# Where the output projection's products stand: moving six units' share into the last attention unit's steps

## The chip, the cores and the metric

The kernel runs on one core of a Trainium2 chip. The metric is the device time of one execution in microseconds (us). A core has TensorE (matrix products, called PE in the profile; its weight loads are PEld), VectorE (DVE), ScalarE (ACT), GpSimd (POOL) and SyncE (SP), which here only issues transfers. Each engine works through its own queue in order; semaphores hold an instruction until its inputs are there and its output buffer is free.

## The reference

A decoder trunk of two layers over 1024 tokens of width 1024, float32. Layer 1 uses differential attention with 8 heads ("units"), layer 2 forgetting attention with 16 heads (8 units of two heads). Each layer ends in a gated MLP. What matters here is the end of each attention stage: the heads' outputs, side by side, are multiplied by an output matrix, normalised and added to the stream.

```python
# layer 1
o = jnp.concatenate(outs, axis=1)
o = rms_norm(o, subln_g, SUBLN_EPS) * (1.0 - lambda_init)
a = o.reshape(B, S, A_HEADS * 2 * A_HEAD_DIM).astype(x.dtype) @ w_o
h = h + rms_norm(a, a_norm_post[l])
# layer 2
a = o.reshape(B, S, B_HEADS * B_HEAD_DIM).astype(x.dtype) @ w_o
h = h + rms_norm(a, b_norm_post[j])
f = conv_ffn(rms_norm(h, ffn_norm_pre[l]), ffn_w_in[l], ffn_conv_w[l], ffn_conv_b[l], ffn_w_out[l])
h = h + rms_norm(f, ffn_norm_post[l])
```

## The kernel before, in words

**Split products.** A float32 product is made of three products in a faster format (`fp32r`): each operand is split into a high part (a copy, by ScalarE) and a low part (the difference, by VectorE or GpSimd), and high x high, high x low and low x high are summed in PSUM. So a weight or an activation costs one ScalarE copy and one subtraction before it can be used.

**PSUM** has eight banks of 128 x 512 floats. In an attention stage the scores use banks 0 to 3, the transposes 4 and 5; projections and the products with the values ("PV") take the banks in the list `mlast`.

**An attention stage** is a loop over steps, written out by `go`. Layer 1 (`attention_a`) has 64 steps, 8 per unit, one for each block of 128 query rows, smallest first. Layer 2 (`attention_b`) has 128 steps, 8 per head and 16 per unit, the largest block first. In step n the kernel issues: the scores and softmax of block n (`front`), the transposes of block n-2 and their evacuation in two parts (`turn`), in every other step PV for a pair of blocks (`pv`), then filling work (`fill`), then what stands in `todo` for this step. This is program order; a scheduler that works at compile time lays each engine's queue in this order as priority, and brings a later instruction forward where it reckons that an earlier one is not ready.

**The filling work** (`plan`) is the query, key and value projections of later units, in pieces of 12 products 512 wide (`qk_pieces`, line 690) or 24 products 256 wide (`v_pieces`, line 757). Unit 7 is the last; its eight pieces are numbers 72 to 79, and line 902 puts them from step 48 (layer 1) or 96 (layer 2) on: one piece a step in layer 1, steps 49 to 55, and one every two steps in layer 2, steps 96 to 110.

**The output projection** is the products of 8 token blocks (128 rows each) with 8 units' rows of the matrix: per block and unit 6 products 512 wide (three parts, two column halves), 384 in a layer, all at line 464. `output_plan` puts its beginning into `todo`. Here `first` is the last unit's first step (56 in layer 1, 112 in layer 2), `n` the number of steps (64, 128) and `per` the steps of a unit (8, 16).

- `begin` sets `mlast = [4, 5]` and loads the norm's gain.
- `weight` asks for one of the eight weight tiles, evenly over the last unit. A weight is loaded into one of two raw buffers (`wr`), and split into two tiles of the pool `x`. That pool has 16 tiles, and the stage's own transposed input fills all 16 until the last projection has read it.
- The units' outputs lie in DRAM (`o_dram`); `out_load` fetches them for a token block (`oraw`), `out_split` splits them, `out_mm` issues products.
- Block 0 gets its products with units 0 to 5 during the last unit's steps, one unit every `per // 8` steps.
- Blocks 1 to 3 get theirs at step n + 4, behind the last PV in program order, and unit 6's products for blocks 0 to 3 come there too: 108 + 24 products.
- The last unit's own output goes through a reciprocal (layer 1: a norm), a row written to DRAM, that row read back to all partitions, and a scaling (`a_norm`, lines 1051 to 1071; `b_scale`, lines 1217 to 1235). It stays on the chip (`o_last`).
- `output_rest` then goes through the 8 blocks: unit 7's products for blocks 0 to 3, all 48 products for blocks 4 to 7. `post` follows for each block: square, gain, norm, addition to the stream; and after the later blocks the transposes for the MLP.

Of the kernel before, what the change touches and what calls it, by code (L numbers as in the profile page):

```python
# [95 lines left out]
class Kernel:  # L96
# [310 lines left out]
    def output_plan(self, gpost, h_in, h_out, gain, n, per):  # L407


        nc = self.nc  # L410
        self.todo = {}
        o = self.out_state = {"w": [], "raw": {}, "part": {}}

        def begin():
            self.mlast = [4, 5]
            o["post"] = self.make_post(gpost, h_in, h_out, False)

        def weight():
            o["w"].append(self.w.next(far=1))

        at = lambda step, *f: self.todo.setdefault(step, []).extend(f)
        first = n - per
        at(first, begin)
        for k in range(8):
            at(first + k * per // 8, weight)
        for tb in range(4):
            at(first + per // 4, lambda tb=tb: self.out_load(tb, 0, 6))
        eng = nc.gpsimd if per == NB else nc.vector
        at(first + 3 * per // 8, lambda: self.out_split(0, 0, 6, eng))
        for j in range(6):  # L430
            at(first + (3 + j) * per // 8, lambda j=j: self.out_mm(0, j, j + 1))
        at(n - 2, *[lambda tb=tb: self.out_load(tb, 6, 7) for tb in range(4)])
        for tb in range(1, 4):
            at(n - 2 + tb, lambda tb=tb: self.out_split(tb, 0, 6, nc.gpsimd))
        at(n + 4, *[lambda tb=tb: self.out_split(tb, 6, 7, nc.vector) for tb in range(4)])
        at(n + 4, *[lambda tb=tb: self.out_mm(tb, 0, 6) for tb in range(1, 4)])
        at(n + 4, *[lambda tb=tb: self.out_mm(tb, 6, 7) for tb in range(4)])

    def out_load(self, tb, c0, c1):
        r = self.out_state["raw"]  # L440
        if tb not in r:
            r[tb] = self.tile("oraw", shape=[P, 7, P])
        self.nc.sync.dma_start(
            out=r[tb][:, c0:c1], in_=self.o_dram[c0:c1, :, tb * P:(tb + 1) * P].rearrange("h p t -> p h t")
        )

    def out_split(self, tb, c0, c1, eng):
        nc, s = self.nc, self.out_state
        if tb not in s["part"]:
            s["part"][tb] = tuple(self.tile("o" + n, F32R, [P, 8, P], tag="w") for n in "hl")  # L450
        oh, ol = s["part"][tb]
        src = self.o_last[:, tb * P:(tb + 1) * P].unsqueeze(1) if c0 == 7 else s["raw"][tb][:, c0:c1]
        nc.scalar.copy(out=oh[:, c0:c1], in_=src)
        eng.tensor_tensor(out=ol[:, c0:c1], in0=src, in1=oh[:, c0:c1], op=ALU.subtract)

    def out_mm(self, tb, j0, j1):
        nc, s = self.nc, self.out_state
        oh, ol = s["part"][tb]
        b = 2 * ((tb + 3) % 4)
        for j in range(j0, j1):  # L460
            wh, wl = s["w"][j]
            for i, (o, wt) in enumerate(((oh, wh), (oh, wl), (ol, wh))):
                for c in range(2):
                    nc.tensor.matmul(  # L464
                        self.bank(b + c), o[:, j], wt[:, 0, c * HALF:(c + 1) * HALF],
                        start=j == 0 and i == 0, stop=j == 7 and i == 2,
                    )

    def output_rest(self, gain):
        nc, s = self.nc, self.out_state  # L470
        self.x_tag = "t"
        for tb in range(NB):
            if tb + 4 < NB:
                self.out_load(tb + 4, 0, 7)
            if tb < 4:
                self.out_split(tb, 7, 8, nc.vector)
                self.out_mm(tb, 7, 8)
            else:
                self.out_split(tb, 0, 7, nc.vector)
                self.out_split(tb, 7, 8, nc.vector)  # L480
                self.out_mm(tb, 0, 8)
            s["raw"].pop(tb)
            s["part"].pop(tb)
            if tb == 5:
                self.w.make(self.w.used + 2)
            s["post"](tb, self.ps[:, 2 * ((tb + 3) % 4) * HALF:2 * ((tb + 3) % 4) * HALF + D])
            if tb > 4:
                self.early(gain, tb - 4, (6, 0, 2))
        self.mlast = [6, 7]


# [389 lines left out]
    def plan(self, n_steps, start, layer_b):  # L881

        out = {}
        last = -1
        per = n_steps // 4
        pre = 4 if layer_b else 0
        for p in range(4):
            f = []
            for u in (2 * p + 1, 2 * p + 2):
                if u < 8:  # L890
                    f.append((u, None))
            if p < 3:
                f.append((None, p + 1))
            for i in range(8 * len(f)):
                u, v = f[i // 8]
                k = 24 * p + i
                if k < pre:
                    step = -1
                elif k < 72:
                    step = start + (k - pre) * 3 * per // (72 - pre)  # L900
                else:
                    step = 3 * per + (k - 72) * per // 16
                last = max(last, step)
                out.setdefault(last, []).append((u, v, i % 8))
        made = {}

        def emit(step):
            for u, v, i in out.get(step, []):
                if (u, v) not in made:
                    if u is None:  # L910
                        made[u, v] = self.v_pieces(v, layer_b)
                    else:
                        qk = self.qk_pieces(u)
                        made[u, v] = [x for which in "qk" for half in (0, 1) for x in qk[which, half]]
                made[u, v][i]()

        return emit
# [517 lines left out]
```

## Time and profile before

| What | Value |
|---|---|
| Median of 3 runs | 2557.89 us (2554.6 to 2558.18) |
| Profiled execution | 2557.8 us, of which the span is 2555.9 us |
| TensorE busy | 2495.0 us, 98% |
| VectorE, ScalarE, GpSimd busy | 1628.0, 1145.0, 853.1 us |
| Granted TensorE clock, mean | 0.996 |
| Last two units of layer 1 | about 381 to 487 us from the span's start |
| Last two units of layer 2 | about 1679 to 1798 us |

The page of the profile lists each engine's busy time, then the chain of work that ended last, then the costliest groups of instructions by line. A view by stretch gives the busy time of every engine between two moments; a view of waits says which engine stood idle for whom; a view in order of time lists single instructions with start and length. "L464" is line 464 of the kernel. A product counts as busy from its issue to a modelled end, so a busy TensorE is not a TensorE at its full pace.

### The profile page before, as it was taken

Reading aid. Unit: us, or ns where it says so; the run is one execution under the profiler, and the core shown is the slowest. Engines: PE = TensorE matmul, PEld = TensorE weight load, DVE = VectorE, ACT = ScalarE, POOL = GpSimd, SP = SyncE. Lnnn points to the kernel's source line nnn. Section 1 sums busy time; section 2 is a strip of 40 time slices with the busy share of each in tenths; the row PEclk is TensorE's granted clock in tenths of the full one; section 3 lists DMA queues with packets and bytes.
Section 4 is the critical chain, followed back from the end, with each engine's and each line's share of the span. In section 5 each row is a group of like instructions: output and inputs, shape, how many; then the busy total and the mean of one; then the engine's idle time right before and its main releaser. Section 6 shows DMA issues by size and latency. Waiting matters only on the chain.

```text
span 2555.9 us, 33917 instructions
## 1 busy us (share of the span) xinstructions
PE 2495.0 (98%) x12876; PEld 2118.3 (83%) x12876; DVE 1628.0 (64%) x2334; ACT 1145.0 (45%) x1949; POOL 853.1 (33%) x1057
## 2 busy tenths in 40 slices
PE   8999999999999999999999999997999999999998
PEld 8898998788788888888878888885887888888887
DVE  6767676568777877252556666666468777775243
ACT  5555555455333434242445555556344443434231
POOL 1222222226554550010334444435236455430000
PEclk9999999999999999999999999999999999999999
DMA  4111211441222225363311212224412222235363
GB/s 166 44 44 45 62 52 47 132 163 57 85 90 83 74 93 197 108 210 119 119 59 50 59 59 63 69 37 128 145 66 99 83 75 98 76 116 182 123 206 115
DMA packets 119864, 248.98 MB, mean 97 GB/s; under 512 B 34035, under 2 KB 50196, under 8 KB 119700
## 3 DMA queue, kind: packets, MB, share of 16 engines
q1 hardware_dynamic: 119700, 246.81, 29.5%
q8 instruction: 101, 1.65, 0.3%
q14 instruction: 63, 0.52, 0.1%
HBM read 197.85 MB, written 48.92 MB: 97 GB/s over the span
## 4 chain that ended last, share of the span: by engine, by line
PE 85%; DVE 7%; ACT 2%; DMA 2%; issue 2%; POOL 1%; SPq 0%; DVEq 0%; ACTq 0%; POOLq 0%
PE ps L581 28%; PE ps L293 18%; PE ps L690 13%; PE ps L757 7%; PE ps L464 6%; PE ps L836 3%; PE ps L1207 2%; PE ps L1035 2%; PE ps L806 2%; PE ps L805 2%; PE ps L565 1%; DVE y L612 1%; DVE wl L81 1%; DVE tl L555 1%; DMA wr<-in_b_o_dram 1%
## 5 line engine op out<-in xcount | busy, mean ns | idle before, releaser
L81 DVE TENSOR_TENSOR wl<-wr,wh 128x1024 fp32r<-128x1024 f32 x160 | 202.6, 1267 | 282.2 <-ACT wh L79 275.7
L293 PE MATMUL ps<-wh,src 128*128 128x512 f32 x1408 | 377.2, 389 | 0.0
L79 ACT CAST wh<-wr 128x1024 fp32r<-128x1024 f32 x164 | 172.2, 1052 | 337.2 <-PE ps L293 238.4
L293 PEld LDWEIGHTS ps<-wh,src 128*128 128x128 f32 x1408 | 264.1, 188 | 55.1 <-issue 0.2
L581 PE MATMUL ps<-xq,sh 128*128 128x512 f32 x912 | 281.3, 390 | 2.0 <-ACT e L589 2.0
L610 ACT ACTIVATE y<-ps,conv 128x1024 f32<-128x1024 f32 x88 | 106.2, 1207 | 370.9 <-DVE ps L586 369.0
L612 DVE SCALAR_TENSOR_TENSOR y<-ps,conv,y 128x1023 f32<-128x1023 f32 (+1 forms) x176 | 224.8, 1278 | 55.1 <-ACT y L610 51.2
L293 PE MATMUL ps<-wl,src 128*128 128x512 f32 x704 | 216.8, 389 | 0.0
L817 POOL CAST qz<-qs 64x128 fp32r<-64x128 f32 x256 | 82.6, 324 | 391.2 <-PE ps L806 340.3
L210 POOL TENSOR_SCALAR post<-post 128x1 f32<-128x1 f32 x56 | 21.4, 382 | 569.0 <-ACT f L214 568.6
L690 PE MATMUL ps<-xh,wh 128*128 128x512 f32 x512 | 207.4, 405 | 1.4 <-DVE qs L711 0.7
L516 POOL TENSOR_TENSOR sl<-ws,sh 128x1024 fp32r<-128x1024 f32 x38 | 105.5, 2776 | 303.2 <-ACT sh L515 303.2
L581 PEld LDWEIGHTS ps<-xq,sh 128*128 128x128 f32 x912 | 170.9, 188 | 38.6 <-ACT e L589 3.4
L690 PE MATMUL ps<-xh,wl 128*128 128x512 f32 x512 | 201.2, 393 | 0.0
L690 PE MATMUL ps<-xl,wh 128*128 128x512 f32 x512 | 201.2, 393 | 0.0
L847 DVE TENSOR_TENSOR ptl<-ps,pth 128x512 fp32r<-128x512 f32 (+3 forms) x288 | 152.6, 553 | 65.8 <-ACT pth L846 64.5
L581 PE MATMUL ps<-th,sh 128*128 128x512 f32 x456 | 177.6, 390 | 2.0 <-DVE f L586 2.0
L581 PE MATMUL ps<-tl,sh 128*128 128x512 f32 x456 | 177.4, 389 | 0.0
L581 PE MATMUL ps<-xq,sl 128*128 128x512 f32 x456 | 177.4, 389 | 0.0
L581 PE MATMUL ps<-th,sl 128*128 128x512 f32 x456 | 177.4, 389 | 0.0
L846 ACT CAST pth<-ps 128x512 fp32r<-128x512 f32 (+3 forms) x288 | 130.5, 478 | 60.7 <-PE ps L836 56.5
L293 PEld LDWEIGHTS ps<-wl,src 128*128 128x128 f32 x704 | 132.2, 188 | 27.3
(197 smaller groups left out, 6152.3 us busy)
## 6 DMA issues: line engine op xcount, KB each, us to landing
wr<-in_ffn_in_dram SPq DMA_DIRECT2D x88, 512.0 KB, 3.5
wr<-in_ffn_out_dram SPq DMA_DIRECT2D x88, 512.0 KB, 3.6
g<-y SPq DMA_DIRECT2D x44, 512.0 KB, 2.8
g<-g SPq DMA_DIRECT2D x44, 512.0 KB, 6.6
h<-hold SPq DMA_DIRECT2D x24, 512.0 KB, 2.9
hold<-h SPq DMA_DIRECT2D x24, 512.0 KB, 6.8
crow<-c SPq DMA_DIRECT2D x16, 512.0 KB, 8.4
xraw<-in_x_dram SPq DMA_DIRECT2D x8, 512.0 KB, 6.6
```

What stands on the lines that cost most here:

```text
L79: self.k.nc.scalar.copy(out=hi[:, :size], in_=raw[:, :size])
L81: eng.tensor_tensor(out=lo[:, :size], in0=raw[:, :size], in1=hi[:, :size], op=ALU.subtract)
L293: nc.tensor.matmul(self.bank(2 * t + c), s[:, sp, t * P:(t + 1) * P], wt[:, 0, c * HALF:(c + 1) * HALF], start=first and wt is wh and sp = ...
L464: nc.tensor.matmul(self.bank(b + c), o[:, j], wt[:, 0, c * HALF:(c + 1) * HALF], start=j == 0 and i == 0, stop=j == 7 and i == 2,)
L516: (eng or nc.vector).tensor_tensor(out=lo, in0=raw, in1=hi, op=ALU.subtract)
L581: nc.tensor.matmul(o, w[wi][:, k], x[k][xi], start=start and k == 0 and i == 0, stop=k == 3 and i == 2, skip_group_check=not start,)
L610: nc.scalar.activation(out=y, in_=ps, func=AF.Identity, scale=cw[:, 2:3], bias=cw[:, 3:4])
L612: nc.vector.scalar_tensor_tensor(out=y[:, k:], in0=ps[:, :S - k], scalar=cw[:, 2 - k:3 - k], in1=y[:, k:], op0=ALU.mult, op1=ALU.add)
L690: nc.tensor.matmul(self.bank(b), w[:, kc], x[kc][:, c], start=kc == 0 and i == 0, stop=kc == 7 and i == 2)
L757: nc.tensor.matmul(o, x[kc][:, tb * P:(tb + 1) * P], w[:, kc % 4], start=kc == 0 and i == 0, stop=kc == 7 and i == 2,)
L846: nc.scalar.copy(out=hi, in_=src)
L847: nc.vector.tensor_tensor(out=lo, in0=src, in1=hi, op=ALU.subtract)
```

## The change

Three things are changed, in both layers.

1. **Unit 7's projections** are made two pieces at a time: the divisor at line 902 goes from 16 to 32. They end at step 51 in layer 1 and at step 103 in layer 2.
2. **Blocks 0 to 3 with units 0 to 5** are now 16 groups of 18 products (`out_part`: a block, a column half, three units). All are summed in bank 7; after the second group of a column half ScalarE copies the bank into a tile `osum`. In layer 1 two groups go to each of the steps 59 to 66, in layer 2 one to each of 112 to 127. `begin` comes three or seven steps ahead of the last unit and leaves PV bank 6 alone. Weights are asked for at given steps: six of them by step 57 in layer 1, five by step 111 and six by step 112 in layer 2. The loads of blocks 0 to 3 go into tiles of the pool `x`, all four at step 57 in layer 1, one to a step from 107 to 110 in layer 2. The splits are GpSimd's in layer 1 and VectorE's in layer 2, where blocks 1 to 3 were GpSimd's.
3. **Behind the last PV**, at step n + 4, only block 4 is issued ahead, with units 0 to 6 (42 products). In `output_rest` blocks 0 to 3 get the products of units 6 and 7 (12 each) in another bank pair, and VectorE adds `osum`. Units 6 and 7 of these blocks are split 512 columns at a time.

```diff
     def output_plan(self, gpost, h_in, h_out, gain, n, per):
...
         def begin():
-            self.mlast = [4, 5]
+            self.mlast = [6]
             o["post"] = self.make_post(gpost, h_in, h_out, False)
 
         def weight():
-            o["w"].append(self.w.next(far=1))
+            o["w"].append(self.w.next(far=2))
...
         first = n - per
-        at(first, begin)
-        for k in range(8):
-            at(first + k * per // 8, weight)
+        wide = per == NB
+        eng = self.nc.gpsimd if wide else self.nc.vector
+        step = lambda b, x: first + (x if wide else b)
+        at(step(-7, -3), begin)
+        for j, b, x in ((0, -7, -3), (1, -6, -3), (2, -4, -2), (3, -3, -1), (4, -1, 0), (5, 0, 1), (6, 7, 5), (7, 11, 7)):
+            at(step(b, x), weight)
         for tb in range(4):
-            at(first + per // 4, lambda tb=tb: self.out_load(tb, 0, 6))
-        eng = nc.gpsimd if per == NB else nc.vector
-        at(first + 3 * per // 8, lambda: self.out_split(0, 0, 6, eng))
-        for j in range(6):
-            at(first + (3 + j) * per // 8, lambda j=j: self.out_mm(0, j, j + 1))
-        at(n - 2, *[lambda tb=tb: self.out_load(tb, 6, 7) for tb in range(4)])
-        for tb in range(1, 4):
-            at(n - 2 + tb, lambda tb=tb: self.out_split(tb, 0, 6, nc.gpsimd))
-        at(n + 4, *[lambda tb=tb: self.out_split(tb, 6, 7, nc.vector) for tb in range(4)])
-        at(n + 4, *[lambda tb=tb: self.out_mm(tb, 0, 6) for tb in range(1, 4)])
-        at(n + 4, *[lambda tb=tb: self.out_mm(tb, 6, 7) for tb in range(4)])
+            at(step(-5 + tb, 1), lambda tb=tb: self.out_load(tb, 6, "x"))
+        for tb, b, x in ((0, -2, 2), (1, 3, 3), (2, 6, 5), (3, 10, 6)):
+            at(step(b, x), lambda tb=tb: self.out_split(tb, 6, eng))
+        for i in range(16):
+            at(step(i, 3 + i // 2), lambda i=i: self.out_part(i // 4, i // 2 % 2, i % 2))
+        at(n - 1 if wide else n - 4, self.out_load_last)
+        at(n if wide else n - 2, lambda: self.out_load(4, 7, "t"))
+        at(n + 4, lambda: self.out_split_last(0))
+        at(n + 4, lambda: self.out_split(4, 7, self.nc.vector))
+        at(n + 4, lambda: self.out_mm(4, 0, 7))
...
+    def out_part(self, tb, c, third):
+        nc, s = self.nc, self.out_state
+        oh, ol = s["part"][tb]
+        for j in range(3 * third, 3 * third + 3):
+            self.out_products(7, (oh[:, j], ol[:, j]), j, c, j == 0, j == 5)
+        if third == 0:
+            return
+        if c == 0:
+            s["sum"][tb] = self.tile("osum")
+        nc.scalar.copy(out=s["sum"][tb][:, c * HALF:(c + 1) * HALF], in_=self.bank(7))
+        if c == 1:
+            s["part"].pop(tb)
+
+    def out_bank(self, tb):
+        return (6, 4, 6, 4, 0, 2, 6, 4)[tb]
...
     def output_rest(self, gain):
...
+        self.out_split_last(1)
         for tb in range(NB):
-            if tb + 4 < NB:
-                self.out_load(tb + 4, 0, 7)
+            b = self.out_bank(tb)
+            ps = self.ps[:, b * HALF:b * HALF + D]
+            if tb in (1, 2, 3):
+                self.out_load(tb + 4, 7, "t")
             if tb < 4:
-                self.out_split(tb, 7, 8, nc.vector)
-                self.out_mm(tb, 7, 8)
+                oh, ol = s["late"]
+                t = slice(tb * P, (tb + 1) * P)
+                for j in (6, 7):
+                    for c in range(2):
+                        self.out_products(b + c, (oh[:, j - 6, t], ol[:, j - 6, t]), j, c, j == 6, j == 7)
+                o = s["sum"].pop(tb)
+                nc.vector.tensor_tensor(out=o, in0=ps, in1=o, op=ALU.add)
+                ps = o
             else:
-                self.out_split(tb, 0, 7, nc.vector)
-                self.out_split(tb, 7, 8, nc.vector)
-                self.out_mm(tb, 0, 8)
+                if tb > 4:
+                    self.out_split(tb, 7, nc.vector)
+                    self.out_mm(tb, 0, 7)
+                self.out_split_one(tb)
+                self.out_mm(tb, 7, 8)
...
@@ plan
-                    step = 3 * per + (k - 72) * per // 16
+                    step = 3 * per + (k - 72) * per // 32
```

More of the change, by code (lines that the diff above doesn't have):

```diff
@@ L407, in output_plan @@
     def output_plan(self, gpost, h_in, h_out, gain, n, per):
-        nc = self.nc
         self.todo = {}
-        o = self.out_state = {"w": [], "raw": {}, "part": {}}
+        o = self.out_state = {"w": [], "raw": {}, "part": {}, "sum": {}}
         def begin():
-            self.mlast = [4, 5]
+            self.mlast = [6]
             o["post"] = self.make_post(gpost, h_in, h_out, False)
         def weight():
-            o["w"].append(self.w.next(far=1))
+            o["w"].append(self.w.next(far=2))
@@ L432, in output_plan @@
-        at(n - 2, *[lambda tb=tb: self.out_load(tb, 6, 7) for tb in range(4)])
-        for tb in range(1, 4):
-            at(n - 2 + tb, lambda tb=tb: self.out_split(tb, 0, 6, nc.gpsimd))
-        at(n + 4, *[lambda tb=tb: self.out_split(tb, 6, 7, nc.vector) for tb in range(4)])
-        at(n + 4, *[lambda tb=tb: self.out_mm(tb, 0, 6) for tb in range(1, 4)])
-        at(n + 4, *[lambda tb=tb: self.out_mm(tb, 6, 7) for tb in range(4)])
[L439 to L442, printed above, removed]
+        wide = per == NB
@@ new lines, in output_plan, with out_load @@
+        for i in range(16):
[5 more added lines that the diff above has]
+        at(n + 4, lambda: self.out_mm(4, 0, 7))
+    def out_load(self, tb, n, tag):
+        r = self.out_state["raw"][tb] = self.tile("oraw", shape=[P, n, P], tag=tag)
@@ L443, in out_load, with out_split @@
         self.nc.sync.dma_start(
-            out=r[tb][:, c0:c1], in_=self.o_dram[c0:c1, :, tb * P:(tb + 1) * P].rearrange("h p t -> p h t")
+            out=r, in_=self.o_dram[0:n, :, tb * P:(tb + 1) * P].rearrange("h p t -> p h t")
         )
-    def out_split(self, tb, c0, c1, eng):
+    def out_split(self, tb, n, eng):
         nc, s = self.nc, self.out_state
[L449 to L454, printed above, removed]
@@ L456, in out_mm, with out_split_one @@
-    def out_mm(self, tb, j0, j1):
+        src = s["raw"].pop(tb)
+        oh, ol = s["part"][tb] = tuple(self.tile("o" + x, F32R, [P, 8, P], tag="w") for x in "hl")
+        nc.scalar.copy(out=oh[:, :n], in_=src)
+        eng.tensor_tensor(out=ol[:, :n], in0=src, in1=oh[:, :n], op=ALU.subtract)
+    def out_split_one(self, tb):
+        nc = self.nc
+        oh, ol = self.out_state["part"][tb]
+        src = self.o_last[:, tb * P:(tb + 1) * P]
+        nc.scalar.copy(out=oh[:, 7], in_=src)
+        nc.vector.tensor_tensor(out=ol[:, 7], in0=src, in1=oh[:, 7], op=ALU.subtract)
@@ new lines, in out_load_last, with out_split_last @@
+    def out_load_last(self):
+        r = self.out_state["raw6"] = self.tile("oraw6", shape=[P, HALF])
+        self.nc.sync.dma_start(out=r, in_=self.o_dram[6, :, 0:HALF])
+    def out_split_last(self, i):
+        nc, s = self.nc, self.out_state
+        if i == 0:
+            s["late"] = tuple(self.tile("o" + x, F32R, [P, 2, HALF], tag="w") for x in "hl")
+        oh, ol = s["late"]
+        src = s.pop("raw6") if i == 0 else self.o_last[:, 0:HALF]
+        nc.scalar.copy(out=oh[:, i], in_=src)
+        nc.vector.tensor_tensor(out=ol[:, i], in0=src, in1=oh[:, i], op=ALU.subtract)
@@ L457, in out_mm, with out_products @@
+    def out_products(self, bank, o, j, c, start, stop):
+        wh, wl = self.out_state["w"][j]
+        oh, ol = o
+        for i, (x, wt) in enumerate(((oh, wh), (oh, wl), (ol, wh))):
+            self.nc.tensor.matmul(
+                self.bank(bank), x, wt[:, 0, c * HALF:(c + 1) * HALF], start=start and i == 0, stop=stop and i == 2
+            )
+    def out_part(self, tb, c, third):
         nc, s = self.nc, self.out_state
         oh, ol = s["part"][tb]
-        b = 2 * ((tb + 3) % 4)
@@ L460, in out_mm @@
-        for j in range(j0, j1):
[L461 to L467, printed above, removed]
+        for j in range(3 * third, 3 * third + 3):
+            self.out_products(7, (oh[:, j], ol[:, j]), j, c, j == 0, j == 5)
@@ new lines, in out_part, with out_mm @@
+        if third == 0:
[7 more added lines that the diff above has]
+        return (6, 4, 6, 4, 0, 2, 6, 4)[tb]
+    def out_mm(self, tb, j0, j1):
+        oh, ol = self.out_state["part"][tb]
+        for j in range(j0, j1):
+            for c in range(2):
+                self.out_products(self.out_bank(tb) + c, (oh[:, j], ol[:, j]), j, c, j == 0, j == 7)
@@ L471, in output_rest @@
         self.x_tag = "t"
+        self.out_split_last(1)
         for tb in range(NB):
-            if tb + 4 < NB:
-                self.out_load(tb + 4, 0, 7)
+            b = self.out_bank(tb)
+            ps = self.ps[:, b * HALF:b * HALF + D]
+            if tb in (1, 2, 3):
+                self.out_load(tb + 4, 7, "t")
             if tb < 4:
-                self.out_split(tb, 7, 8, nc.vector)
-                self.out_mm(tb, 7, 8)
-            else:
-                self.out_split(tb, 0, 7, nc.vector)
-                self.out_split(tb, 7, 8, nc.vector)
-                self.out_mm(tb, 0, 8)
-            s["raw"].pop(tb)
-            s["part"].pop(tb)
+                oh, ol = s["late"]
+                t = slice(tb * P, (tb + 1) * P)
+                for j in (6, 7):
+                    for c in range(2):
+                        self.out_products(b + c, (oh[:, j - 6, t], ol[:, j - 6, t]), j, c, j == 6, j == 7)
+                o = s["sum"].pop(tb)
+                nc.vector.tensor_tensor(out=o, in0=ps, in1=o, op=ALU.add)
+                ps = o
+            else:
+                if tb > 4:
+                    self.out_split(tb, 7, nc.vector)
+                    self.out_mm(tb, 0, 7)
+                self.out_split_one(tb)
+                self.out_mm(tb, 7, 8)
+                s["part"].pop(tb)
+            if tb == 3:
+                s.pop("late")
             if tb == 5:
                 self.w.make(self.w.used + 2)
-            s["post"](tb, self.ps[:, 2 * ((tb + 3) % 4) * HALF:2 * ((tb + 3) % 4) * HALF + D])
+            s["post"](tb, ps)
             if tb > 4:
-                self.early(gain, tb - 4, (6, 0, 2))
+                self.early(gain, tb - 4, (0, 2, 6))
         self.mlast = [6, 7]
```

## The prediction

> **What bounds the kernel now.** I read the page's busy line first, then the chain, then busy time by stretch around the end of each attention stage, the only place that the diff touches.
>
> ```profile
> span 2555.9 us, 33917 instructions
> PE 2495.0 (98%) x12876; PEld 2118.3 (83%) x12876; DVE 1628.0 (64%) x2334; ACT 1145.0 (45%) x1949; POOL 853.1 (33%) x1057
> PE 85%; DVE 7%; ACT 2%; DMA 2%; issue 2%; POOL 1%; SPq 0%; DVEq 0%; ACTq 0%; POOLq 0%
> ```
>
> TensorE is busy for all but 61 us, and the change keeps the number of products (8 blocks x 8 units x 3 x 2 = 384 per layer). It can gain only idle TensorE time, and loses wherever it opens some. I cut the first layer by steps: 49-51 (390.3-412.5), 52-58 (to 450.6), 59-63 (to 479.6), tail; and the second: 104-111, 112-118, 119-127. Columns: length, then PE, PEld, DVE, ACT and POOL busy, granted clock, DMA share, GB/s.
>
> ```profile
> 390.30:412.50 22.20, 22.20 (x140) 19.97 (x139) 10.20 (x29) 8.94 (x23) 2.66 (x9) 1.00 0.00 1
> 412.50:450.60 38.10, 35.14 (x219) 30.50 (x219) 34.16 (x75) 25.47 (x57) 14.22 (x32) 1.00 0.33 100
> 450.60:479.60 29.00, 24.52 (x121) 18.80 (x120) 25.28 (x51) 20.93 (x43) 13.78 (x17) 1.00 0.63 169
> 509.30:564.80 55.50, 55.50 (x263) 46.31 (x262) 35.29 (x43) 28.26 (x50) 15.65 (x28) 1.00 0.52 181
> ...
> 1708.90:1738.80 29.90, 26.36 (x151) 21.43 (x150) 21.08 (x42) 19.23 (x40) 18.00 (x29) 1.00 0.47 90
> 1738.80:1767.70 28.90, 16.98 (x93) 13.04 (x93) 16.15 (x33) 18.01 (x36) 15.23 (x28) 0.94 0.63 177
> 1767.70:1800.00 32.30, 31.84 (x183) 25.41 (x182) 18.17 (x46) 17.83 (x45) 12.85 (x27) 1.00 0.28 55
> ```
>
> The reader is to see three things. Idle TensorE time here is 3.0 + 4.5 us in the first layer and 3.5 + 11.9 + 0.5 us in the second: 23 us, the whole prize. In the first layer VectorE is the engine beside it (34.16 of 38.10, 90%). In the second no engine is full in 1738.8-1767.7; there ScalarE stood in its queue for transfers:
>
> ```profile
> ACT wh L79 <- DMA wr<-in_b_o_dram: 4.9, 3, 2.2
> ACT oh L453 <- DMA oraw<-o_b: 3.6, 2, 2.5
> ```
>
> **The change, part by part.** *The price of a 512-wide product*: in a run of 21 back to back the first and last start at
>
> ```profile
> 394.83 0.40 PE L690 MATMUL ps<-xh,wh 128*128 128x512 f32 x1
> 399.37 0.39 PE L690 MATMUL ps<-xh,wl 128*128 128x512 f32 x1
> ```
>
> so 4.54/20 = 0.227 us each. The busy view books 0.39, so every stall hides up to 0.16 us.
>
> *Projections twice as dense, first layer.* Unit 7's last four pieces leave steps 52-55 for 49-51. The stretch 390.3-412.5 is all TensorE (22.20 of 22.20) and grows by what moves in. What leaves:
>
> ```profile
> 412.50:450.60 38.10, 12.10 (x48) 8.66 (x48) 1.00 0.33 100
> 412.50:450.60 38.10, 4.89 (x4) 0.00 (x0) 1.00 0.33 100
> 1735.39 0.68 DVE L719 TENSOR_TENSOR kl<-ps,kh 64x512 fp32r<-64x512 f32 x1
> ```
>
> 48 projection products (first row, line 690) = 10.9 us. VectorE there holds 34.16 us; two evacuations of two 0.68 us instructions go (-2.7) and six weight splits instead of four (second row, line 81: 4.89/4 = 1.22) come (+2.4): 33.9 us. TensorE keeps 35.14 - 10.9 = 24.2. So VectorE paces steps 52-58 and the fill that ran under it for nothing is gone. At 90 to 95% VectorE, I take 36.6 us: idle 12.4 instead of 3.0, **+9.4**. Bounds: 33.9 us flat (+6.7) and the old 38.1 (+10.9). The four block loads leave together at step 57, and ScalarE's queue must wait for the first before softmax can go on; four together cost it 3.6 us in the second layer (waits above): 0 to 3.6, **+1**.
>
> *Products into steps 59-66.* 16 groups of 18 products, 4.1 us each, two groups a step: 8.2 us beside some 5 us of VectorE per step (25.28/5). TensorE has always something to do: the 4.5 idle and 2 hidden (an estimate: a dozen stalls of up to 0.16) go, **-6.5**. Each pair of groups ends in a ScalarE copy of bank 7, nearest row
>
> ```profile
> 482.57 0.59 ACT L846 CAST pth<-ps 128x512 fp32r<-128x512 f32 x1
> ```
>
> and the next group waits for it; scores and transposes of the next step stand between, so nothing. PV has bank 6 alone, two steps apart: nothing.
>
> *First tail: "only the fifth block".* The last PV must travel through norm, DRAM row and scale before unit 7's products can start:
>
> ```profile
> 486.80 0.28 PE L1035 MATMUL ps<-pth,v 128*128 128x256 f32 x1
> 489.49 0.17 DVE L1055 SCALAR_TENSOR_TENSOR sta<-ps,sta 128x8 f32<-128x8 f32 x1 [4.75 <-PE ps L1051]
> 489.81 1.65 POOL L1058 TENSOR_TENSOR sta<-sta,mhalf 128x8 f32<-128x8 f32 x1 [17.28 <-DVE sta L1055]
> 491.48 0.38 SPq L858 DMA_DIRECT2D r_a<-sta  x1
> 501.90 0.33 SPq L1065 DMA_DIRECT2D r<-r_a  x1
> 507.38 1.29 DVE L1071 SCALAR_TENSOR_TENSOR o<-o,subg,r 128x1024 f32<-128x1024 f32 x1 [17.72 <-DMA r<-r_a]
> 509.03 0.90 DVE L454 TENSOR_TENSOR ol<-o,oh 128x128 fp32r<-128x128 f32 x4 [0.37 <-ACT oh L453]
> ```
>
> From 487.1 to 509.3 it is 22.2 us, 10.4 of them the row's write before SP may issue the read; SP's later loads (blocks 6 to 8) queue behind that read as they do now. Today 132 products (30 us) cover it. After: 42 of the fifth block, 12 of unit 6 for two blocks (the third shares banks with the first), and the last two groups (36) as far as they stand behind that PV: 54 to 90 products, 12.3 to 20.4 us. Exposed 1.8 to 9.9; the groups follow the PV in program order, so nearer the low end: **+3**.
>
> *Second tail.* Its chain starts at the reciprocal, which needs no PV:
>
> ```profile
> 1793.53 0.20 DVE L1217 RECIPROCAL stb<-stb 128x8 f32<-128x8 f32 x1
> 1794.30 8.37 SPq L1230 DMA_DIRECT2D r<-r_b  x2
> 1807.41 1.23 DVE L1235 TENSOR_TENSOR o<-o,r 128x1024 f32<-128x1024 f32 x1 [8.97 <-DMA r<-r_b]
> 1809.01 0.90 DVE L454 TENSOR_TENSOR ol<-o,oh 128x128 fp32r<-128x128 f32 x4 [0.37 <-ACT oh L453]
> ```
>
> 15.8 us against 18 + 54 products (16.3) and the last transposes and PV: 0 to 4, **+1**.
>
> *Second layer, steps 104-111.* Again 48 products (line 690) leave,
>
> ```profile
> 1708.90:1738.80 29.90, 12.65 (x48) 8.64 (x48) 1.00 0.47 90
> 1732.98 2.36 POOL L81 TENSOR_TENSOR wl<-wr,wh 128x1024 fp32r<-128x1024 f32 x1 [1.60 <-ACT wh L79]
> 1763.41 0.96 DVE L454 TENSOR_TENSOR ol<-oraw,oh 128x768 fp32r<-128x768 f32 x1 [1.80 <-ACT oh L453]
> wr<-in_b_o_dram SPq DMA_DIRECT2D x8, 512.0 KB, 3.5
> oraw<-o_b SPq DMA_DIRECT2D x4, 384.0 KB, 6.2
> ```
>
> so TensorE keeps 15.5 us. Five weights and the first block's split now fall here: POOL 18.0 + 2.4 = 20.4 us, VectorE 21.08 - 2.7 + 0.96 = 19.3. Floor 20.4/0.9 = 22.7 us. Ceiling: today's unfilled stretch, 28.9 us for seven steps, 33 for eight. Of that ScalarE waited 8.5 us for transfers; these come one to a step now and the four block loads no longer in a burst, but five at 3.5 and four at 6.2 us still share the stretch. I take 25: idle 9.5 instead of 3.5, **+6**; ends +3.7 and +14.
>
> *Steps 112-127.* One group (4.1 us) per step against VectorE's 34 us in sixteen steps: TensorE paces it. Idle 11.9 + 0.5 falls to 1 (**-11.4**), and with it the clock's loss in that stretch (0.06 x 28.9 = 1.7) and some hidden 2.3: **-4**.
>
> *After the tails.* Blocks 1 to 4 need one more VectorE instruction each, nearest
>
> ```profile
> 515.43 1.22 DVE L353 TENSOR_TENSOR f<-ps,gpost 128x1024 f32<-128x1024 f32 x1
> ```
>
> +4.9, less the fifth block's split (1.09): 35.29 becomes 39 us, in 186 products and the transposes, 46 us: 85% where it was 64%. VectorE at 90% went with 3.0 us idle in 412.5-450.6, so **+1** per layer, 0 to 3.
>
> *Sum.* First layer +9.4 + 1 - 6.5 + 3 + 1 = +7.9; second +1 + 6 - 11.4 - 4 + 1 = -7.4. Total +0.5 on the profiled execution's 2557.8 (span 2555.9 and 1.9 around it), which stands at the median 2557.89: **2558**. A measurement of this kernel can tell a change of about 0.2%, 5 us, from none.
>
> **The rivals.** *Second layer's gain kept, first layer's cost small* (faster). VectorE runs steps 52-58 without gaps (+6.7), the first tail is covered (0), steps 104-111 take the floor 22.7 us (+3.7 instead of +6), second tail 0: 2.7 + 3 + 2.3 + 1 = 9 better; no wait for the loads (1) and nothing after the tails (2) make 12: 2546. For: VectorE has 10.20 of 22.20 us before step 52, so it starts with no backlog. Against: 25.28 of 29.00 is its best pace when only it is short.
>
> *The first tail decides* (slower). If the last two groups run ahead of the last PV while its probabilities are turned and copied, and the unit 6 products queue behind the first wait on unit 7, 42 products (9.5 us) face 22.2: +12.7 instead of +3. It decides from 98 products (22.2/0.227) downward. A long stall also takes the clock, as at 1738.8-1767.7 (0.94, 1.7 us): 2558 + 9.7 + 1.7 = 2569; half way to the ceiling in steps 104-111 (+4) makes 2573. The Trainium skill, "TensorE: Matmul & The Clock Gate" ("What's actually happening"), says that TensorE drops to half clock after an idle window of about 3.4 us; by that rule a 12 us stall costs a further 1.7 us (an estimate: half of the window), a 3 us one nothing. The trace agrees so far: the one lowered clock lies where the idle is.
>
> *The change does not do what it says.* Weights late for step 112 (two raw buffers, 3.5 us each plus a split): the groups wait and the idle only moves from 112-118: of the 15.4 gained there 11 are gone, 2569. Against: five of eight are asked for before step 112.
>
> **How the numbers follow.** Balance as summed 0.45 (own range 2550 to 2566; 0.28 within 0.2%, 0.09 faster, 0.08 slower); faster rival 0.30 (2546); first tail 0.20; late weights 0.05. Faster 0.39, same 0.28, slower 0.33. The range takes in both rivals and the bounds of the two unfilled stretches: 2541 to 2572.
>
> **What would show it.** Idle TensorE time of 8 to 13 us just before the products begin in each layer, with VectorE near 90% in the first; no idle from the first group to the last; a gap of 1 to 5 us before unit 7's first product in the first layer, under 4 in the second; granted clock 1.00 where 0.94 stood. I am wrong upward if a tail gap is over 6 us, downward if steps 52-58 or 104-111 run within 2 us of the floors.

## The result, and the profile after

The changed kernel takes 2594.66 us (median of 4 runs, 2588.42 to 2595.50) against 2557.77 for the kernel before (4 runs on the same chip): ratio 1.0136, 95% interval 1.0123 to 1.0149. It is 37 us slower where 2558 was forecast. The execution that was profiled is the fastest of the four, 2588.42, at a clock of 0.990 where the others had 0.986 or 0.987; what follows accounts for its 30.4 us of longer span, not for the last 6 of the median.

The busy line and the chain by engine:

```profile
span 2586.3 us, 33912 instructions
PE 2502.5 (97%) x12876; PEld 2126.6 (82%) x12876; DVE 1643.2 (64%) x2333; ACT 1151.7 (45%) x1953; POOL 855.0 (33%) x1054
PE 83%; DVE 7%; DMA 3%; ACT 2%; issue 2%; POOL 1%; SPq 0%; DVEq 0%; POOLq 0%; ACTq 0%
```

TensorE is busy 7.5 us longer for the same 12876 matmuls, and idle 83.8 us instead of 60.9. The stretches that answer to those of the prediction, cut at the same steps of the kernel (length, then PE, PEld, DVE, ACT and POOL busy, granted clock, DMA share, GB/s): steps 49-51; 52-58; 59 to the last PV; the first tail (last PV to unit 7's first product); from there to the FFN's first product; then the second layer's steps 104-111, 112 to the last PV, tail, and behind the tail:

```profile
390.00:423.20 33.20, 33.20 (x187) 29.10 (x186) 15.16 (x36) 13.35 (x29) 4.42 (x12) 1.00 0.06 20
423.20:455.10 31.90, 23.93 (x142) 20.10 (x142) 28.86 (x66) 21.03 (x48) 14.70 (x26) 0.89 0.46 147
455.10:507.90 52.80, 49.44 (x267) 42.09 (x267) 30.05 (x58) 27.12 (x56) 15.79 (x19) 0.97 0.26 76
507.90:532.50 24.60, 16.85 (x83) 13.85 (x82) 1.49 (x3) 1.94 (x5) 1.65 (x1) 0.95 0.22 63
532.50:593.90 61.40, 52.64 (x226) 42.67 (x227) 38.99 (x43) 27.14 (x48) 16.16 (x28) 0.88 0.45 160
1744.00:1772.60 28.60, 22.01 (x121) 18.14 (x120) 22.04 (x40) 19.13 (x39) 18.82 (x31) 0.88 0.63 203
1772.60:1832.90 60.30, 58.34 (x343) 50.39 (x342) 36.59 (x78) 36.22 (x82) 21.38 (x49) 1.00 0.26 69
1832.90:1844.50 11.60, 9.65 (x43) 7.64 (x43) 1.78 (x3) 1.16 (x4) 0.00 (x0) 1.00 0.46 121
1844.50:1904.60 60.10, 50.79 (x228) 41.08 (x228) 38.85 (x43) 27.21 (x48) 15.88 (x28) 0.91 0.46 162
```

A stretch's *excess* below is its length less the time that its matmuls take back to back at full clock, 0.227 us for 512 columns, 0.171 for 384, 0.120 for 256 and 0.109 for 128 and fewer (the spacing of undisturbed starts in the trace). It counts idle time and slow clock together, and lets stretches with different work be compared.

| stretch | excess before | after | moved by | forecast |
|---|---|---|---|---|
| steps 52-58 | 4.8 | 12.8 | +8.0 | +10.4 |
| 59 to the last PV | 7.0 | 6.1 | -0.9 | -6.5 |
| first tail | 0.1 | 7.9 | +7.8 | +3 |
| behind the first tail | 0.1 | 14.2 | **+14.1** | **+1** |
| steps 104-111 | 5.8 | 11.4 | +5.6 | +6 |
| 112 to the last PV | 19.1 | 3.7 | -15.4 | -15.4 |
| second tail | 0 | 2.0 | +2.0 | +1 |
| behind the second tail | 0 | 12.9 | **+12.9** | **+1** |

They add to +34.1. The stretch between, from the FFN's first product to step 96, ran 3.4 us shorter (1110.8 us against 1114.2) for a reason that no run here isolates. The attention steps came out near their forecast in all but one row, and together 2.7 us better than before. The loss is in the tails and above all behind them, where before TensorE had no idle time at all (55.50 of 55.50). What TensorE waits for from 507.9 to 593.9 (in total, times, longest), and those instructions:

```profile
PE ps L480 <- ACT oh L473: 7.8, 1, 7.8
PE ps L222 <- DVE f L353: 6.5, 1, 6.5
PE ps L480 <- DVE ol L451: 1.3, 1, 1.3
PE ps L222 <- DVE f L372: 1.0, 1, 1.0
```
```profile
532.48 0.80 PE L480 MATMUL ps<-wh,oh 128*128 128x512 f32 x1 [7.75 <-ACT oh L473]
...
546.23 0.39 PE L480 MATMUL ps<-wl,oh 128*128 128x512 f32 x1
553.13 0.90 PE L222 MATMUL ps<-ident,f 128*128 128x128 f32 x3 [6.51 <-DVE f L353]
554.98 0.90 PE L222 MATMUL ps<-ident,f 128*128 128x128 f32 x3 [0.95 <-DVE f L372]
557.17 1.22 PE L480 MATMUL ps<-wh,ol 128*128 128x512 f32 x2 [1.30 <-DVE ol L451]
```

The first row is the tail. The others: at 546.23 TensorE has issued the first four products of block 5 (the two of each half that need only `oh`). Next in its queue stand transposes for the MLP (line 222). They go to PSUM bank 0, which block 4 holds until its gain product (551.86) has read it. Then comes the product with `ol`, block 5's difference (line 451). VectorE meanwhile:

```profile
547.73 1.22 DVE L523 TENSOR_TENSOR osum<-ps,osum 128x1024 f32<-128x1024 f32 x1
...
550.72 1.22 DVE L353 TENSOR_TENSOR f<-osum,gpost 128x1024 f32<-128x1024 f32 x1
551.86 1.22 DVE L353 TENSOR_TENSOR f<-ps,gpost 128x1024 f32<-128x1024 f32 x1
554.17 0.75 DVE L372 TENSOR_SCALAR f<-hold,post 128x1024 f32<-128x1024 f32 x1 [1.10 <-POOL post L211]
554.84 1.28 DVE L363 SCALAR_TENSOR_TENSOR hold<-f,post,hold 128x1024 f32<-128x1024 f32 x1
556.03 1.08 DVE L451 TENSOR_TENSOR ol<-oraw,oh 128x896 fp32r<-128x896 f32 x1
```

Behind the unit's output blocks 0 to 4 have 54 products left, some 13 us here; the rows that they release cost VectorE four additions, five gain products, and the second and third steps of each block. The split of block 5 is queued behind nearly all of it, at 556.03. In the kernel before, the split of the next block came ahead of all gain products, and 133 products stood between the unit's output and the first transposes:

```profile
514.42 1.09 DVE L454 TENSOR_TENSOR ol<-oraw,oh 128x896 fp32r<-128x896 f32 x1 [4.49 <-ACT oh L453]
...
539.54 1.04 PE L222 MATMUL ps<-ident,f 128*128 128x128 f32 x8
```

After the change VectorE is busy for 9.07 of the 10 us in which TensorE runs dry, and the clock falls to half behind that:

```profile
540.00:550.00 10.00, 6.62 (x30) 5.14 (x28) 9.07 (x10) 6.18 (x10) 4.89 (x8) 1.00 0.53 175
550.50:560.80 10.30, 5.42 (x15) 3.86 (x16) 8.49 (x10) 5.79 (x10) 4.88 (x8) 0.50 0.70 256
```

So the 14.2 us are 8.8 us of waiting (61.40 - 52.64, the last three waits) and 5.4 of products run slowly (52.64 busy for 47.2 of work, at a mean clock of 0.88).

### The profile page after: what moved, and what is told of

Same layout as the page of the kernel before. It is cut to its first block, busy times and chain, and to the rows that moved or that the text cites. A ratio compares the mean times of both kernels' runs of the same rounds, so it can differ in the third digit from the quotient of the medians.

```text
span 2586.3 us, 33912 instructions
## 1 busy us (share of the span) xinstructions
PE 2502.5 (97%) x12876; PEld 2126.6 (82%) x12876; DVE 1643.2 (64%) x2333; ACT 1151.7 (45%) x1953; POOL 855.0 (33%) x1054
## 4 chain that ended last, share of the span: by engine, by line
PE 83%; DVE 7%; DMA 3%; ACT 2%; issue 2%; POOL 1%; SPq 0%; DVEq 0%; POOLq 0%; ACTq 0%
PE ps L631 27%; PE ps L293 18%; PE ps L740 13%; PE ps L807 7%; PE ps L480 5%; PE ps L886 3%; PE ps L1257 2%; PE ps L1085 2%; PE ps L856 2%; PE ps L855 2%; PE ps L615 1%; DVE y L662 1%; DMA r_a<-sta 1%; DVE wl L81 1%; DVE tl L605 1%
```

## The experiments

Blocks are counted from 0 in this text; the fifth, sixth, seventh and eighth block of the prediction and the expectations are blocks 4 to 7. "Behind" is the excess behind the output of the unit, first and second layer.

| run | median us | ratio, 95% interval | first tail | behind |
|---|---|---|---|---|
| the change | 2594.66 | 1.0136 (1.0123 to 1.0149) | 7.9 | 14.2, 12.9 |
| e1 projections alone | 2579.08 | 1.0079 (1.0063 to 1.0096) | 0.2 | 0, 0 |
| e2 two blocks ahead | 2580.99 | 1.0090 (1.0072 to 1.0107) | 1.4 | 12.4, 12.1 |
| e3 last groups late | 2592.03 | 1.0127 (1.0112 to 1.0142) | 4.8 | 14.9, 13.0 |
| e4 second layer alone | 2564.73 | 1.0022 (1.0012 to 1.0031) | 0.3 | 0, 13.8 |
| e5 e2 + transposes behind | 2589.40 | 1.0120 (1.0106 to 1.0134) | 1.8 | 16.0, 15.7 |
| e6 e5 + split ahead | 2567.85 | 1.0034 (1.0020 to 1.0047) | 0.1 | 6.0, 6.9 |
| e7 no additions | 2570.11 | 1.0044 (1.0030 to 1.0058) | 7.8 | 3.0, 2.4 |
| e8 e4 mended as e6 | 2554.28 | 0.9985 (0.9976 to 0.9993) | 0.1 | 0.1, 5.6 |
| e9 order only | 2576.83 | 1.0064 (1.0051 to 1.0078) | 8.0 | 6.8, 6.6 |
| e10 e6, no additions | 2554.32 | 0.9979 (0.9970 to 0.9988) | 0 | 0.5, 0.4 |
| e11 e8, transposes midway | 2555.20 | 0.9979 (0.9969 to 0.9988) | 0.2 | 0, 5.5 |
| e12 e6, thin projections in layer 1 | 2568.20 | 1.0033 (1.0021 to 1.0046) | 0 | 6.8, 5.7 |

Each ratio is to the kernel before on the same chip: 2558.73 us for e1 to e4, 2559.02 for e5 to e8, 2559.57 for e9 to e12.

**e1: the dense projections alone.** The kernel before, with one number changed:

```diff
-                    step = 3 * per + (k - 72) * per // 16
+                    step = 3 * per + (k - 72) * per // 32
```

> The kernel before, with unit 7's projections twice as dense and nothing else changed. Theory A (the loss lies behind the last PV: too few products stand there against the row's way through DRAM and against VectorE's work for five blocks at once): the dense projections alone cost only what steps 52-58 and 104-111 lose, 8.0 + 5.7 us by excess over product time, less the idle that the old late fill finds: 5 to 14 us, so 2563 to 2572. Theory B (the dense projections are the main cause, by opening the unfilled steps and cooling the clock): 20 us or more, 2578 or above.

2579.08 us: 20 us for this part by itself, theory B's number. Steps 52-58 have an excess of 15.2 (before 4.8), 59 to the last PV 11.4 (7.0), steps 104-111 18.8 (5.8), and 112 to the last PV still 13.3; both tails and what follows them stay without excess. So the room that is made costs 20 us and must be refilled. The change refills it: in the second layer the groups take 13.3 to 3.7, and all the stretches ahead of the tails end 2.7 us better than before. So theory A, which missed the number of this run, has the place of the change's loss right.

**e2: block 5 ahead as well.** Its load, split and 42 products join block 4's at step n + 4:

```diff
-        at(n if wide else n - 2, lambda: self.out_load(4, 7, "t"))
+        for tb in (4, 5):
+            at(n if wide else n - 2, lambda tb=tb: self.out_load(tb, 7, "t"))
...
+        at(n + 4, lambda: self.out_split(5, 7, self.nc.vector))
         at(n + 4, lambda: self.out_mm(4, 0, 7))
+        at(n + 4, lambda: self.out_mm(5, 0, 7))
...
```

> The changed kernel, with the sixth block (load, split and its 42 products with units 0 to 6) issued ahead beside the fifth. Theory A: 9.5 us of products fill the waits before unit 7's first product (7.9 us in the first layer, 2.4 in the second), and the sixth block's split no longer stands behind VectorE's work for blocks 1 to 5, so of the 14.3 and 12.5 us lost behind the tails about 9 go in each: 25 us faster than the changed kernel (15 to 32), 2562 to 2580. Theory B: only the tails' 10 us can go, 2585 or above.

2580.99 us. The 42 products (9.5 us) take the first tail from 7.9 to 1.4 and the second from 2.0 to nothing: the tails were short of products. The excess behind hardly moves (12.4, 12.1), though block 5's split is out of the way: the transposes still wait for block 4's gain product, now until 558.12, and block 6's split stands behind that product, at 562.09. TensorE's waits from 509.8 to 586.0 (the second row is the tail's):

```profile
PE ps L222 <- DVE f L353: 9.7, 2, 9.4
PE ps L483 <- ACT oh L476: 1.2, 1, 1.2
```

**e3: the last two groups behind the norm.**

```diff
-            at(step(i, 3 + i // 2), lambda i=i: ...
+            at(n + 4 if wide and i > 13 else step(i, 3 + i // 2), lambda i=i: ...
```

> The changed kernel, with the last two of the 16 groups in the first layer issued at step n + 4, behind the norm's small products, instead of at step 66. Theory A: 36 more products (8.2 us) cover the row's way and the norm does not wait 4 us for a group: the 7.9 us wait in the first layer goes, what is lost behind it stays: 6 to 9 us faster than the changed kernel, 2586 to 2589. Theory B: no change within 3 us.

2592.03 us. The tail goes from 7.9 to 4.8, but the stretch ahead of the last PV from 6.1 to 8.3: the transposes' wait there is 3.7 us where it was 3.0, and the granted clock 0.94 where it was 0.97. So the two groups had been worth something where they stood, and less was won than expected.

**e4: the second layer alone changed.** The first layer keeps the plan, the loads, the splits and the divisor 16 of before.

> The first layer as in the kernel before, the second as in the changed one. By the two traces the first layer lost 29 us and the second 5, so both theories give 5 us over the kernel before if the parts add up: 2560 to 2568. If the first layer's delay was partly made good further on (3 us were, at the start of the second layer), 2563; over 2575 would mean that the second layer pays for something of its own that the trace of one execution does not show.

2564.73 us, as expected. The second layer alone costs 6 us; by difference the first layer makes the other 30.

**e5 and e6: the transposes' place, then the split's.** The queue orders are the planner's, not the source's, so the first edit fixes one of them. `issue_after` keeps order on one queue and adds no wait; `self.put` is the latest product.

```diff
-            if tb > 4:
-                self.early(gain, tb - 4, (0, 2, 6))
+            if tb > 5:
+                with self.tc.issue_after(self.put.ins):
+                    self.early(gain, tb - 5, (0, 2, 6))
+        self.early(gain, 3, (0, 2, 6))
```

> The fifth and the sixth block go ahead of the first four, as in the second experiment (2580.99 us), and the first eight of the MLP's transposes are put behind the seventh block's 48 products on TensorE's queue, the next eight behind the eighth's. Theory C (the transposes' place on TensorE's queue alone makes the loss behind the unit's output): the excess there falls from 12.4 and 12.1 us to 5 or less each, and the time to 2564 to 2569 us. Theory C2 (VectorE's queue: the seventh block's split stands in it behind the work of the first five blocks as well, so the wait only goes from the transposes to the products): the excess stays at 10 to 13 us each, 2577 to 2582 us, and the row with the long wait names the seventh block's difference. Theory D (VectorE has too much to do there): the same as C2.

2589.40 us, 8 more than e2, and 16.0 and 15.7 behind. The waits go to the seven-unit splits of blocks 6 and 7 (line 453 is the copy on ScalarE; 7.6 and 3.1 us); from 535.7 to 588.9:

```profile
PE ps L483 <- ACT oh L453: 10.7, 2, 7.6
PE ps L483 <- ACT oh L476: 1.6, 1, 1.6
PE ps L483 <- DVE ol L454: 0.9, 1, 0.9
```

Theory C falls: the transposes had been done inside a wait that was there anyway, and held back they come on top. C2 had 2577 to 2582 and missed that too; it also named VectorE's difference, where the row names the copy, which stood in ScalarE's queue behind the squares of finished blocks. For e6 block 6's split goes ahead of the first four blocks, and GpSimd takes the differences of blocks 6 and 7:

```diff
-        for tb in (4, 5):
+        for tb in (4, 5, 6):
...
         self.out_split_last(1)
+        self.out_split(6, 7, nc.gpsimd)
         for tb in range(NB):
...
```

> As the run before, and besides the seventh block is loaded with the fifth and sixth and its seven units are split by ScalarE and GpSimd ahead of the first four blocks' work, the eighth block's difference is GpSimd's too. VectorE's work there falls by two differences of 1.1 us. Theory C2: now nothing that TensorE needs next stands behind the five blocks' work on VectorE; the excess falls to 2 to 5 us in each layer and the time to 2560 to 2567 us. Theory C: no change against the run before but for a us or two. Theory D: 2 us less in each layer, 2574 to 2579 us.

2567.85 us: 21.6 less than e5, with excesses of 6.0 and 6.9. VectorE's busy time there is 36.35 us, where e5 had 35.40 in a longer stretch: the loss went and the load did not. The two differences that GpSimd took over are worth 2 us a layer by theory D, of 10.0 and 8.8 won. No run moved the split and left the transposes where the change has them. What is left from 533.6 to 577.6 is one wait for block 3's scaled rows:

```profile
533.60:577.60 44.00, 40.31 (x187) 32.99 (x185) 36.35 (x38) 24.36 (x44) 23.81 (x31) 0.96 0.57 201
```
```profile
PE ps L222 <- DVE f L372: 3.6, 1, 3.6
```

About half of this wait seems to be the edit's own. That scaling, at 559.90, took 2.56 us where line 372 takes 0.75 elsewhere, and GpSimd's split of block 7 ran beside it, from 558.98 for 2.93 us.

**e7: without the additions.**

```diff
-                o = s["sum"].pop(tb)
-                nc.vector.tensor_tensor(out=o, in0=ps, in1=o, op=ALU.add)
-                ps = o
+                s["sum"].pop(tb)
```

> The changed kernel (2594.66 us) without the four additions of the kept sums (it leaves units 0 to 5 out of blocks 0 to 3 of both layers). VectorE has 4.9 us less to do behind each unit's output. Theory D (load): both excesses, 14.2 and 12.9 us, fall by 5 us each and more, 2582 to 2585 us. Theory C or C2 (order and bunching): the additions are part of the bunch, so it ends earlier by what of them lies ahead of the fifth block's gain product, 3 to 5 us a layer, 2585 to 2589 us, and 8 us or more of each excess stay.

This kernel leaves units 0 to 5 out of the results of blocks 0 to 3, though their products are made. 2570.11 us: 24.6 less than the change, twice what any theory said. Behind the first tail, no wait is left:

```profile
532.80:582.90 50.10, 50.10 (x227) 41.34 (x228) 34.25 (x39) 27.10 (x48) 15.88 (x28) 0.95 0.56 196
```
```profile
545.71 1.08 DVE L451 TENSOR_TENSOR ol<-oraw,oh 128x896 fp32r<-128x896 f32 x1
```

VectorE's 4.7 us less work is not the size of the 11.2 and 10.5 that come back. Without the additions the planner ordered two queues otherwise: block 5's split is at 545.71 in place of 556.03, and its 48 products stand ahead of the transposes. The run tells load from order no better than before.

**e9: the order alone.** The change with all its additions and one block ahead, but with the orders that e7 had:

```diff
...
+                if tb == 3:
+                    a, d = self.out_split(5, 7, nc.vector)
+                    with self.tc.issue_after(a.ins), self.tc.issue_after(d.ins):
+                        nc.vector.tensor_tensor(out=o, in0=ps, in1=o, op=ALU.add)
+                        s["post"](tb, o)
...
             if tb > 4:
-                self.early(gain, tb - 4, (0, 2, 6))
+                with self.tc.issue_after(self.put.ins):
+                    self.early(gain, tb - 4, (0, 2, 6))
```

> The changed kernel (2594.66 us) with all its additions and only one block ahead. Two orders are put in by hand, those that the run without the additions had: the sixth block's split stands on ScalarE and VectorE ahead of the fourth block's addition and gain product, and each set of eight transposes stands on TensorE behind the products of the sixth, the seventh and the eighth block. VectorE does as much as in the changed kernel. Theory C2 (what TensorE needs next stands behind the bunch in the queues): the excess behind the output falls from 14.2 and 12.9 us to 3 to 6 each, 2575 to 2581 us. Theory D (the additions' load on VectorE is the loss, the order an accompaniment): the excess stays at 10 or more each, 2587 to 2593 us.

2576.83 us, 17.8 less than the change, as theory C2 said; D's 2587 to 2593 is out. VectorE does what it did (38.86 us; 38.99 in the change); the split is at 547.13:

```profile
531.90:585.80 53.90, 50.28 (x227) 40.99 (x228) 38.86 (x43) 27.25 (x48) 20.73 (x28) 0.96 0.52 181
```
```profile
547.13 1.08 DVE L451 TENSOR_TENSOR ol<-oraw,oh 128x896 fp32r<-128x896 f32 x1
```

The excesses are 6.8 and 6.6, a little above the 3 to 6 expected. Nearly the same queue order with the additions (e9) and without (e7) differs by 3.8 and 4.2 us: that is the additions' own price, and the order's is 7.4 and 6.3.

**e10: e6 without the additions.**

> The version with two blocks ahead, the seventh block's split ahead and the transposes behind the seventh block's products (2567.85 us), without the four additions of the kept sums (units 0 to 5 are missing from blocks 0 to 3 of both layers). It had 6.0 and 6.9 us of excess left behind the output; its longest wait there is the transposes' for the fourth block's scaled rows, 3.6 us. Theory C2 with the bunch: the additions lie ahead of those rows, so 4.9 us less work there takes the wait away, the excess falls to 1 to 3 us each, 2557 to 2562 us. Rival (what is left is the row chain's own latency and the clock): it stays at 5 or more each, 2566 to 2569 us.

It leaves out what e7 leaves out. 2554.32 us, under the 2557 to 2562 expected; excesses of 0.5 and 0.4. Behind the first tail TensorE runs through at full clock:

```profile
533.40:571.60 38.20, 38.20 (x185) 31.72 (x183) 31.82 (x34) 23.97 (x44) 19.32 (x31) 1.00 0.64 225
```

With e6 this prices the additions at 5.5 and 6.5 us there. The long scaling is there too (2.61 us beside GpSimd's split), but it comes early enough and TensorE does not wait for it.

**e8 and e11: versions that beat both kernels.** e8 is the second layer alone, mended as e6; e11 puts the first eight transposes between 24 and 24 of block 7's products.

> The first layer as before the change, the second as changed (2564.73 us together), with the second layer mended as in the run before last: two blocks ahead, the seventh block's split ahead, the transposes behind the seventh block's products. Theory C2: the 2.0 us of the tail and 9 to 11 us of the 13.8 behind the output go, 2551 to 2555 us, under the kernel before (2558). Theory D: 2 us of the tail and 2 behind the output go, 2560 to 2562 us. Theory C: as C2 if the seventh block's split hardly matters.

2554.28 us, ratio 0.9985 (0.9976 to 0.9993): faster than the kernel before by 0.15%, in the range of C2. The tail's 2.0 went and 8.2 of the 13.8 behind, a little less than C2 had.

> The mended second layer of the run before (2554.28 us; 5.6 us of excess left behind the output), with the first eight transposes behind 24 of the eighth block's products and not ahead of them all. Theory C2: the transposes' wait of some 3.5 us is covered by 5.4 us of products, the excess falls to 2 to 3 us, 2550.5 to 2552.5 us. Rival: the 24 transposes and their evacuations behind the last block then stand closer together and give it back, 2553.5 to 2556 us.

2555.20 us, ratio 0.9979 (0.9969 to 0.9988): the intervals of the two overlap, and the excess is 5.5 against 5.6, so the step won nothing. In e8 TensorE waited 3.4 us for block 3's scaled rows; in e11 that wait is gone and the next in line has come forth, block 7's split, which takes GpSimd 2.91 us where VectorE took 1.08. First e8's wait from 1823.3 to 1872.3, then e11's from 1826.1 to 1875.1, and the split:

```profile
PE ps L222 <- DVE f L372: 3.4, 1, 3.4
```
```profile
PE ps L567 <- POOL ol L538: 2.6, 1, 2.6
PE ps L567 <- ACT oh L537: 0.8, 1, 0.8
```
```profile
1857.07 2.91 POOL L538 TENSOR_TENSOR ol<-oraw,oh 128x896 fp32r<-128x896 f32 x1
```

**e12: thin projections in the first layer.** The edit is that of e1 undone for layer 1 on the base of e6.

> The version of 2567.85 us with the first layer's projections as thin as before the change (two steps' worth for one), so that they share steps 59 to 63 with the output's products. Theory F (in the first layer the dense projections are the loss: steps 52 to 58 are paced by VectorE whatever TensorE has to do): the excess of steps 52 to 58 goes from 12.3 back to 5 us, that of the steps from 59 to the last group stays at 4 to 8, and the time is 2558 to 2562 us. Theory G (what steps 52 to 58 win is lost behind step 59, since the output's products then come too late and stand behind the last group): 2566 to 2570 us.

2568.20 us: no different from e6, as theory G had it. Steps 52-58 keep an excess of 13.5, now over 43.5 us, and the steps from 59 on have 8.6. Spread or dense, the projections leave the first layer's attention as slow with the output's products as it is in the change.

## Why the prediction was wrong

**What failed: "After the tails ... +1 per layer, 0 to 3".** Measured +14.1 and +12.9. The work was counted rightly: VectorE was to have 39 us there and has 38.99 and 38.85. The inference from it was not. The step took a share of VectorE over the whole stretch and the idle time that went with such a share elsewhere. It is 64% of the longer stretch, yet it is 91% from 540 to 550, where TensorE's 54 products end. Before the change the row work of blocks 0 to 3 stood beside unit 7's 24 products and the 96 of blocks 4 and 5; now that of five blocks stands beside 54 in all. The runs show the loss as 7.4 and 6.3 us of queue order (e9) and 3.8 to 6.5 of the additions (e7 against e9, e10 against e6), slow clock included in each. The order is that of two queues together, the split's place and the transposes'; the one without the other was tried only in e5, which was slower. The remainder, 3.0 and 2.4 in e7, is mostly slow clock behind the tails' stalls: TensorE there hardly waits and has a clock of 0.95 and 0.97. Other PSUM banks for the transposes were not tried.

**"First tail: +3" (1.8 to 9.9).** Measured 7.8, inside the bounds, too near the lower one. Its chain was 24.6 us, not 22.2: the planner put a group of 18 products ahead of the norm's own matmuls, which holds the chain up for the 4.11 us that it covers (other links were shorter).

```profile
507.90 4.11 PE ps L480 x18
512.00 1.69 PE ps L1101 x16
515.73 10.25 DMA r_a<-sta
526.04 4.37 DMA r<-r_a
532.48 2.94 PE ps L480 x6
```

That was the low end of products, about 60 behind the PV (4.1 us of group and 9.5 of block 4). The rival "the first tail decides" had the right sign; its 12.7 was too much, and it would have left the main loss unnamed. (Its upper end of 2573 also lay just outside the range, 2541 to 2572, that was to take it in.)

**"Products into steps 59-66: -6.5".** Measured -0.9. The groups were there to fill the idle time, but 3.4 us stayed idle (52.80 - 49.44), and 2.7 more went inside the busy time, at a clock of 0.97. Most of the idle time is one wait, a transpose's for VectorE's difference of the probabilities:

```profile
PE ps L886 <- DVE ptl L897: 3.0, 1, 3.0
```

e3 and e12 changed which products stand there and had 8.3 and 8.6. Why the first layer's steps don't fill as the second's do stays open.

**What held.** Steps 52-58 +8.0 for +9.4 and 1 for the loads; steps 104-111 +5.6 for +6. These two are partly luck: both were forecast as idle time, but idle time grew by 5.0 and 3.1 alone. The rest lies inside TensorE's busy time, at clocks of 0.89 and 0.88 that the forecast did not have. Steps 112-127 with the clock -15.4 for -15.4; the second tail +2.0, in its bounds of 0 to 4. TensorE was idle 8.0 us in 423.2-455.1 with VectorE at 90% (28.86 of 31.90), as the last part foresaw; in the second layer 6.6 us lies under its 8; and "wrong upward if a tail gap is over 6 us" named one of the two places. "Granted clock 1.00 where 0.94 stood" held for 112 to the last PV, while 0.88 to 0.91 appeared behind both tails and in the steps ahead of the groups.

The clock rule cited from the Trainium skill ("TensorE: Matmul & The Clock Gate", "What's actually happening"), half clock after some 3.4 us of idle, fits the two stalls behind the first output: half clock begins at 530.0, 5.3 us into the 7.75 us that end at 532.48, and at 550.5, 3.9 us into the 6.51 us stall. It does not cover all of the traces. In the kernel before, the half clock of 1751.8 begins inside a wait of 2.3 us. In the changed one half clock also begins at 437.9, where the longest wait nearby is 2.8 us and TensorE had been busy for 1.75 of the last 3.41 us, and at 458.4, where it had been busy for 3.03 of them. My estimate by the rule, 1.7 us for one stall and nothing for a short one, was too small: slow products cost 5.4 us behind the first tail, for in the second half-clock stretch TensorE was still waiting in between (5.42 us busy of 10.30).

## What to carry to other kernels

Work that is moved ahead leaves its consumers behind: before taking products out of a stretch, write down, in each engine's order, what stands in front of the next instruction that the tensor engine needs, and compare that time with the products that are left in front of it. A mean share of an engine hides this; the queue's order in the 15 us around the handover shows it. When such a stretch stalls, the cheap repair is to put the next blocks' splits ahead of the finished blocks' row work, and to hold independent work back only once no wait is left that it could cover.

## What the runs showed of the hardware that I had not expected

The 4 KB row written to DRAM and read back takes 10.25 us before the read starts and 4.37 us more for the read, in the changed kernel as before (10.4): over half of the first tail's 24.6 us, and no edit here shortens it. The write is 1040 packets of 4 bytes. The last that the trace records ends 1.6 us after the issue, and 8.7 us more pass until the landing is signalled; why is not known.

A stall costs more than its length: the half clock that began at 530.0 lasted 6.8 us, and the one at 550.5 lasted 10.2. In these traces half clock comes in pieces of 3.41 us and its multiples, up to 13.65 in e5, but for the last one at each kernel's end.

GpSimd's split of a block, 128x896, takes 2.9 us where VectorE's takes 1.08, and it has a second price. In the five runs that give it block 7's split (e6, e8, e10, e11, e12), the scaling of line 372 that VectorE starts meanwhile takes 2.56 to 2.61 us, eight times in all. Elsewhere that line takes at most 0.79 us.
